# Expert gates by one rounded matmul a token, with the weight split moved to VectorE

## The chip, the cores and the metric

The kernel runs on one core of a Trainium2 chip. Its time is the device time of one execution in microseconds (us). A core has TensorE (PE, with its weight loads as PEld), VectorE (DVE), ScalarE (ACT), GpSimd (POOL) and SyncE (SP, which only issues transfers here). Each engine works through its own instruction list in order and waits on semaphores for the others.

## The reference

Two transformer blocks on 512 tokens of width 1024, in float32. The change lies in the first block's expert layer (`peer`), which selects 16 of 16384 experts for each token and each of 8 heads and mixes them with softmax gates:

```python
def peer(h, w_query, sub_keys, u_tab, v_tab):
    q = rmsnorm((xt @ w_query).reshape(T, PEER_HEADS, 2, PEER_PK_DIM))
    s = jnp.einsum('thpd,pnd->thpn', q, sub_keys)
    s1, i1 = lax.top_k(s[:, :, 0], PEER_TOPK)
    s2, i2 = lax.top_k(s[:, :, 1], PEER_TOPK)
    cand = (s1[..., :, None] + s2[..., None, :]).reshape(T, PEER_HEADS, n_cand)
    cidx = (i1[..., :, None] * PEER_N_KEYS + i2[..., None, :]).reshape(T, PEER_HEADS, n_cand)
    best, pos = lax.top_k(cand, PEER_TOPK)
    eidx = jnp.take_along_axis(cidx, pos, axis=-1)
    gate = jax.nn.softmax(best, axis=-1)
    ...
        act = jax.nn.gelu(jnp.einsum('td,thkd->thk', xb, u_tab[ib])) * gb
        return jnp.einsum('thk,thkd->td', act, v_tab[ib])
```

An expert's number is a pair of keys (i1, i2), each below 128, so one token's gates form a 128 x 128 table with at most 128 filled places.

## The kernel before, in words

The kernel computes the layer densely: gelu(x U) for all 16384 experts, times the token's table of gates, times V. Weights come in slabs of 128 x 2048 float32 (1 MB). `WStream` loads a slab (`wr`, three buffers), ScalarE rounds it (`wh`, line 295, a type whose matmul takes one pass), and a second engine, `lo_eng`, subtracts to get the rest (`wl`, line 302). A product of two float32 matrices is then three rounded matmuls (lines 307 to 309). `get` hands out a slab and splits the one two further on, so in each engine's list the split of slab i+2 stands right before the work of slab i.

The stretch in question is in `phase_peer`, after the queries. 42 of the 64 U slabs (the list `EARLY`) are multiplied there, ahead of the expert stage, and gelu of the result (`he`, line 1282) is stored to `d_h`. Beside them runs `route`, which finds the experts and builds the tables. The rest of the slabs and all V slabs are the stage after it.

`route` is a generator of small steps. `choose(t)` takes 128 tokens: for each of 8 heads a sum of 256 candidates and two rounds of MAX8, FIND_INDEX8 and MATCH_REPLACE8 on VectorE (lines 1463 to 1470), then a look-up of the keys, in which VectorE makes a mask (line 1496), GpSimd multiplies (line 1498) and VectorE reduces (line 1491), and a transpose into `ttt`. `spread(q)` takes four tokens: VectorE writes one one-hot mask for the first key of four tokens in one instruction (`oa`, line 1535) and four masks times gate for the second key (`ob`, line 1537). `place` follows two spreads later: four float32 matmuls into the PSUM tile `psc` (line 1525; a float32 matmul is two passes in the profile, so eight records), and ScalarE copies the 128 x 4 x 128 result into `gs` with the token innermost (line 1526), where consecutive elements of a token lie 128 bytes apart. Eight groups of four fill a 2 MB block that goes to `d_g`.

How the steps mix with the gemms is set by a count. `between` is called eight times a slab; from the 25th call on it takes steps from `route` until the sum of the numbers that they yield reaches its share of a total. 42 slabs are 336 calls. A yielded number is a weight in that share, nothing that is waited for. VectorE does no split in this stretch: `lo_eng` is GpSimd from the queries to the end of `route`.

Of the kernel before, what the change touches and what calls it, by code (L numbers as in the profile page):

```python
# [24 lines left out]
TT = S // 128  # L25
RMS_EPS = 1e-6
DN_ALPHA = 4.0 ** 0.25
EARLY = [i for i in range(64) if i % 4 and i not in (2, 26, 38, 46, 54, 62)]

# [247 lines left out]
class Builder:  # L277
# [913 lines left out]
    def phase_peer(self):  # L1191
# [4 lines left out]
        hh, hl = self.h2h, self.h2l  # L1196
        with ExitStack() as c:
            rp = c.enter_context(self.pool(name="rt_s", bufs=1))
            pp = c.enter_context(self.pool(name="rt_p", bufs=2, space=PSUM))
            iota = rp.tile([128, 128], F32, name="iota")  # L1200
            nc.scalar.dma_start(out=iota, in_=A["iota"])
            val = rp.tile([128, 4, 16, 16], F32, name="val")
# [2 lines left out]
            ws.lo_eng = "pool"  # L1205
            with ExitStack() as cq:
                tp = cq.enter_context(self.pool(name="rt_q", bufs=3))
                kT = rp.tile([128, 2, 128], F32, name="kT")
                nc.scalar.dma_start(out=kT, in_=A["pkT"].rearrange("p (a n) -> p a n", a=2))

                def rank(t, blk, sc):

                    a, b = val[:, t, blk, 0:8], val[:, t, blk, 8:16]
                    nc.vector.max(a, sc)
                    nc.vector.max_index(idx[:, t, blk, 0:8], a, sc)
                    nc.vector.match_replace(sc, a, sc, -3.0e38)
                    nc.vector.max(b, sc)
                    nc.vector.max_index(idx[:, t, blk, 8:16], b, sc)

                def turned(t, qd, q):  # L1220
                    pt = pp.tile([128, 4, 128], F32, name="pt", tag="pt")
                    for b in range(4):
                        nc.tensor.transpose(pt[:, b], q[:, b * 128:(b + 1) * 128], self.ident)
                    qT = tp.tile([128, 4, 128], F32, name="qT", tag="qT")
                    nc.scalar.copy(qT, pt)
                    return t, qd, qT

                def score(t, qd, qT):
                    ps = pp.tile([128, 4, 128], F32, name="psc", tag="psc")
                    for b in range(4):  # L1230
                        nc.tensor.matmul(ps[:, b], qT[:, b], kT[:, b % 2], start=True, stop=True)
                    sc = tp.tile([128, 4, 128], F32, name="sc", tag="sc")
                    nc.scalar.copy(sc, ps)
                    for b in range(4):
                        rank(t, 4 * qd + b, sc[:, b])

                q1, q2 = [], []
                for n in range(18):
                    qd, t = divmod(n, 4)
                    if n < 16:  # L1240
# [16 lines left out]
                    if q2:  # L1257
                        score(*q2.pop())
                    if q1:
                        q2.append(turned(*q1.pop()))  # L1260
                    if n < 16:
                        q1.append((t, qd, q))
            work, total = self.route(c, val, idx, ss, iota, pp)
            hp = c.enter_context(self.pool(name="rt_h", bufs=3))
            spent, n = 0.0, 0

            def between():
# [15 lines left out]
                    nc.sync.dma_start(out=self.d_h[2 * i + m], in_=h)  # L1283
            for _ in work:
                pass
            ws.lo_eng = "dve"
        self.late = ExitStack()
        yp = self.late.enter_context(self.pool(name="ex_y", bufs=1, side="right"))
        y = self.y1 = [yp.tile([128, 1024], F32, name=f"py{t}") for t in range(4)]
# [146 lines left out]
            c = max(a, 1)  # L1436
            nc.vector.tensor_tensor(xx[:, k4, c:b], xT[:, k4, c - 1:b - 1], xT[:, k4, c:b], op=OP.subtract)

    def route(self, ctx, val, idx, ss, iota, pp):


        nc = self.nc
        V, G = nc.vector, nc.gpsimd
        sp = ctx.enter_context(self.pool(name="ro_s", bufs=1))
        gp = ctx.enter_context(self.pool(name="ro_g", bufs=2))
        op_ = ctx.enter_context(self.pool(name="ro_o", bufs=4))
        rs = sp.tile([128, 4, 16], F32, name="rs16")
        nc.scalar.activation(rs, ss, AF.Ln, bias=self.eps_col(RMS_EPS), scale=1.0 / 128)
        nc.scalar.activation(rs, rs, AF.Exp, scale=-0.5)
# [2 lines left out]
        def choose(t):  # L1452
# [50 lines left out]
            for p in pend:  # L1503
                reduce(*p)
            yield 1.2 if t else 16.0
            pt = pp.tile([128, 4, 128], F32, name="pt", tag="pt")
# [3 lines left out]
            V.tensor_copy(tt, pt[:, 0:3])  # L1510
            tts[t] = tt
            yield 0.5

        queue = []
        blocks = {}

        def place():

            q, oa, ob = queue.pop(0)
            if q % 8 == 0:  # L1520
                blocks[q // 8] = gp.tile([128, 128, 32], F32, name="gs", tag="gs")
            gs = blocks[q // 8]
            pg = pp.tile([128, 4, 128], F32, name="psc", tag="psc")
            for r in range(4):
                nc.tensor.matmul(pg[:, r], ob[:, r], oa[:, r], start=True, stop=True)  # L1525
            nc.scalar.copy(gs[:, :, q % 8 * 4:q % 8 * 4 + 4].rearrange("p i t -> p t i"), pg)  # L1526
            if q % 8 == 7:
                nc.sync.dma_start(out=self.d_g[q // 8], in_=blocks.pop(q // 8))

        def spread(q):  # L1530
            tt = tts[q // 32]
            k = q % 32 * 4
            oa = op_.tile([128, 4, 128], F32, name="oa", tag="oa")
            ob = op_.tile([128, 4, 128], F32, name="ob", tag="ob")
            V.tensor_tensor(oa, iota.unsqueeze(1).to_broadcast([128, 4, 128]), tt[:, 0, k:k + 4].unsqueeze(2).to_broadcast([128, 4, 128]), op=OP.is_equal)
            for r in range(4):
                V.tensor_scalar(ob[:, r], iota, tt[:, 1, k + r:k + r + 1], tt[:, 2, k + r:k + r + 1], op0=OP.is_equal, op1=OP.mult)  # L1537
            queue.append((q, oa, ob))
            if len(queue) > 2:
                place()  # L1540

        def steps():
            yield from choose(0)
            for t in range(4):
                nxt = choose(t + 1) if t < 3 else iter(())
                debt = 0.0
                for q in range(32 * t, 32 * t + 32):
                    spread(q)
                    yield 1.65
                    debt += choice / 30  # L1550
                    while debt > 0:
                        d = next(nxt, None)
# [1293 lines left out]
```

## Time and profile before

| | us |
|---|---|
| median of 3 runs (3848.15 to 3857.06) | 3848.38 |
| the profiled execution | 3849.59 |
| its span, first to last instruction | 3847.8 |
| TensorE busy | 3694.6 (96%) |
| VectorE busy | 2321.1 (60%) |
| ScalarE busy | 1502.9 (39%) |
| GpSimd busy | 893.5 (23%) |
| mean granted TensorE clock | 0.984 of full speed |

The profile counts an engine busy from the start to the recorded end of an instruction. Instructions overlap at their ends, so for a sum the distance from one start to the next is the better number, and recorded durations are a little longer than that. The stretch of `route` runs from about 830 to 1408 us of the span.

### The profile page before, as it was taken

To read this page: it belongs to the slowest core of one execution; us is meant where nothing else is said; L and a number is where in the kernel's file an instruction comes from. 1 tells how busy PE (TensorE), PEld (TensorE's weight loads), DVE (VectorE), ACT (ScalarE), POOL (GpSimd) and SP (SyncE) were. 2 spreads that over 40 slices of the span, in tenths; PEclk is the share of its full clock that TensorE was granted. 3 is DMA by queue.
4 is the path that set the end of the run, shared out by engine and by line. 5 is a ranking of instruction groups with operands and counts; after the bars stand their busy time and mean duration, and the time that the engine had idled before them with its cause. 6 is when DMAs were issued, how large, how long until landed. Compare 5 with 4: busy or idle time off the path is not lost.

```text
span 3847.8 us, 49975 instructions
## 1 busy us (share of the span) xinstructions
PE 3694.6 (96%) x19452; PEld 3030.4 (79%) x19456; DVE 2321.1 (60%) x4075; ACT 1502.9 (39%) x2171; POOL 893.5 (23%) x500
## 2 busy tenths in 40 slices
PE   8999999899999999999999998998889998799999
PEld 4788867788888888888888887787778886688887
DVE  3564374696999863443434437873665547856455
ACT  3322284543544543322232324663333324443232
POOL 1201162335443431221221211233420000211000
PEclk9999999999999999999999999999999999899999
DMA  6376564224445566664655643469735221352231
GB/s 251 111 286 194 166 163 145 87 94 153 167 170 177 192 190 180 172 159 140 181 138 157 167 132 122 149 176 269 189 128 150 84 89 67 118 179 99 99 107 58
DMA packets 485884, 582.32 MB, mean 151 GB/s; under 512 B 339824, under 2 KB 381680, under 8 KB 448016
## 3 DMA queue, kind: packets, MB, share of 16 engines
q1 hardware_dynamic: 479744, 568.06, 48.4%
q10 hardware_dynamic: 5904, 11.08, 0.8%
q8 instruction: 153, 2.51, 0.3%
q14 instruction: 83, 0.68, 0.1%
HBM read 456.37 MB, written 121.63 MB: 150 GB/s over the span
## 4 chain that ended last, share of the span: by engine, by line
PE 82%; DVE 11%; ACT 3%; DMA 2%; issue 1%; SPq 1%; POOL 0%; ACTq 0%; DVEq 0%; POOLq 0%
PE acc L307 15%; PE acc L309 15%; PE acc L308 14%; PE pv L307 8%; PE pv L309 8%; PE pv L308 8%; PE psc L1525 3%; PE dpo L2778 1%; PE pz L2075 1%; DVE ob L1537 1%; PE acc L644 1%; PE rps L1833 1%; PE pvp L307 1%; PE pvp L309 1%; PE pvp L308 1%
## 5 line engine op out<-in xcount | busy, mean ns | idle before, releaser
L295 ACT CAST wh<-wr 128x2048 fp32r<-128x2048 f32 (+2 forms) x310 | 510.2, 1665 | 378.2 <-PE pv L309 270.3
L302 DVE TENSOR_TENSOR wl<-wr,wh 128x2048 fp32r<-128x2048 f32 (+2 forms) x236 | 478.6, 2048 | 168.7 <-ACT wh L295 168.5
L308 PE MATMUL pv<-wl,ah 128*128 128x512 f32 x1376 | 535.8, 389 | 1.8 <-DVE wl L302 1.8
L307 PE MATMUL pv<-wh,ah 128*128 128x512 f32 x1376 | 537.0, 390 | 0.4 <-ACT wh L295 0.4
L309 PE MATMUL pv<-wh,al 128*128 128x512 f32 x1376 | 536.0, 390 | 0.0
L302 POOL TENSOR_TENSOR wl<-wr,wh 128x2048 fp32r<-128x2048 f32 (+1 forms) x80 | 333.5, 4176 | 536.7 <-ACT wh L295 508.5
L307 PE MATMUL acc<-h2h,wh 128*128 128x512 f32 x1024 | 412.8, 403 | 0.0
L309 PE MATMUL acc<-h2h,wl 128*128 128x512 f32 x1024 | 402.9, 393 | 0.0
L308 PE MATMUL acc<-h2l,wh 128*128 128x512 f32 x1024 | 399.2, 390 | 0.0
L308 PEld LDWEIGHTS pv<-wl,ah 128*128 128x128 f32 x1376 | 258.6, 188 | 56.4 <-DVE wl L302 2.4
L307 PEld LDWEIGHTS pv<-wh,ah 128*128 128x128 f32 x1376 | 258.6, 188 | 54.7 <-ACT wh L295 0.9
L309 PEld LDWEIGHTS pv<-wh,al 128*128 128x128 f32 x1376 | 258.4, 188 | 54.2
L307 PE MATMUL acc<-xth,wh 128*128 128x512 f32 (+1 forms) x768 | 288.3, 375 | 0.7 <-ACT xth L295 0.7
L309 PE MATMUL acc<-xth,wl 128*128 128x512 f32 (+1 forms) x768 | 286.6, 373 | 0.0
L308 PE MATMUL acc<-xtl,wh 128*128 128x512 f32 (+1 forms) x768 | 284.3, 370 | 1.1 <-DVE xtl L302 1.1
L1376 DVE TENSOR_TENSOR py<-py,pv 128x512 f32<-128x512 f32 x119 | 80.4, 685 | 319.7 <-PE pv L309 319.7
L1537 DVE TENSOR_SCALAR ob<-iota,ttt 128x128 f32<-128x128 f32 x512 | 239.7, 533 | 0.0
L309 PEld LDWEIGHTS acc<-h2h,wl 128*128 128x128 f32 x1024 | 192.1, 188 | 43.1
L1526 ACT COPY gs<-psc 128x512 f32<-128x512 f32 x128 | 143.3, 1120 | 210.5 <-PE psc L1525 207.2
L308 PEld LDWEIGHTS acc<-h2l,wh 128*128 128x128 f32 x1024 | 192.9, 188 | 38.6
L307 PEld LDWEIGHTS acc<-h2h,wh 128*128 128x128 f32 x1024 | 192.9, 188 | 35.4
L302 POOL TENSOR_TENSOR al<-cv,ah 128x512 fp32r<-128x512 f32 x44 | 57.0, 1295 | 633.3 <-ACT ah L295 570.5
(601 smaller groups left out, 7260.4 us busy)
## 6 DMA issues: line engine op xcount, KB each, us to landing
wr<-in_pu SPq DMA_DIRECT2D x64, 1024.0 KB, 5.5
wr<-in_pv SPq DMA_DIRECT2D x64, 1024.0 KB, 5.6
wr<-in_f_up SPq DMA_DIRECT2D x44, 1024.0 KB, 5.0
d_g<-gs SPq DMA_DIRECT2D x16, 2048.0 KB, 10.4
gt<-d_g SPq DMA_DIRECT2D x128, 256.0 KB, 5.7
d_h<-he SPq DMA_DIRECT2D x84, 256.0 KB, 5.3
hs<-d_h SPq DMA_DIRECT2D x84, 256.0 KB, 5.0
wadb<-in_ada_b SPq DMA_DIRECT2D x32, 512.0 KB, 6.4
```

The source lines that it names most:

```text
L295: nc.scalar.copy(hi, src)
L302: (nc.vector if le == "dve" else nc.gpsimd).tensor_tensor(lo, src, hi.bitcast(F32), op=OP.subtract)
L307: mm(ps, w[0], x[0], start=first, stop=False)
L308: mm(ps, w[0], x[1], start=False, stop=False)
L309: mm(ps, w[1], x[0], start=False, stop=last)
L644: nc.tensor.matmul(ps[0:2], sc[:, 4 * half + k], w[:, k], start=(half + k == 0), stop=(half == 1 and k == 3))
L1376: nc.vector.tensor_tensor(yt, yt, ps, op=OP.add)
L1525: nc.tensor.matmul(pg[:, r], ob[:, r], oa[:, r], start=True, stop=True)
L1526: nc.scalar.copy(gs[:, :, q % 8 * 4:q % 8 * 4 + 4].rearrange("p i t -> p t i"), pg)
L1537: V.tensor_scalar(ob[:, r], iota, tt[:, 1, k + r:k + r + 1], tt[:, 2, k + r:k + r + 1], op0=OP.is_equal, op1=OP.mult)
L1833: nc.tensor.matmul(ps[:, i * 256 + hp * 128:i * 256 + hp * 128 + 128], f2(bk[:, 2 * q + i, hp:hp + 2]), ar[:, hp, :, 2 * q + i], start=Tru ...
L2075: nc.tensor.matmul(p[rows[hp], j], l[:, j, h64], r[:, j, h64] if r.shape[2] == 128 else r[:, j], start=True, stop=True)
```

## The change

- `oa` of a token becomes 256 columns of the rounded type: 128 hold the mask of the first key times the gate's rounded part `gh` (four VectorE instructions a group, line 1558), 128 hold the same times the ratio of rest to rounded part (four ScalarE instructions, line 1559). `ob` becomes a plain mask (one VectorE instruction, line 1560). `place` does four rounded matmuls of 256 columns.
- The two halves have to be added. ScalarE copies the low half to `gw` (line 1537), and in the next spread VectorE adds high half and `gw` into `gs` (`gather`, line 1546), in the same layout as before.
- `choose` gets five small VectorE instructions that make `gh` and the ratio.
- In the stretch, `lo_eng` is VectorE; GpSimd keeps only the multiply of the look-up.
- `EARLY` has 45 slabs (26, 46 and 62 are added), so there are 360 calls of `between`; a spread yields 1.9, not 1.65.
- Buffers: `psc` takes two banks a tile and the transposes use `acc`; `oa`, `ob` and `eq` have three buffers, not four, `he` has two, not three.

```diff
-EARLY = [i for i in range(64) if i % 4 and i not in (2, 26, 38, 46, 54, 62)]
+EARLY = [i for i in range(64) if i % 4 and i not in (2, 38, 54)]
...
-            work, total = self.route(c, val, idx, ss, iota, pp)
-            hp = c.enter_context(self.pool(name="rt_h", bufs=3))
+            ws.lo_eng = "dve"
+            work, total = self.route(c, val, idx, ss, iota)
+            hp = c.enter_context(self.pool(name="rt_h", bufs=2))
...
+            gh = sp.tile([128, 128], F32R, name="gh", tag="gh", bufs=2)
+            V.tensor_copy(gh, tt[:, 2])
+            gh = gh.bitcast(F32)
+            gl = sp.tile([128, 16, 16], F32, name="v", tag="v").rearrange("p a k -> p (a k)")[:, 0:128]
+            V.tensor_tensor(gl, tt[:, 2], gh, op=OP.subtract)
+            V.tensor_scalar(tt[:, 2], gh, 1.0e-30, None, op0=OP.max)
+            V.reciprocal(tt[:, 2], tt[:, 2])
+            V.tensor_tensor(tt[:, 2], gl, tt[:, 2], op=OP.mult)
...
             q, oa, ob = queue.pop(0)
+            pg = pp.tile([128, 4, 2, 128], F32, name="psc", tag="psc")
+            for r in range(4):
+                nc.tensor.matmul(pg[:, r], ob[:, r], oa[:, r], start=True, stop=True)
+            lo = op_.tile([128, 4, 128], F32, name="gw", tag="gw", bufs=2)
+            nc.scalar.copy(lo, pg[:, :, 1])
+            sums.append((q, pg, lo))
+
+        def gather():
+
+            q, pg, lo = sums.pop(0)
...
-            pg = pp.tile([128, 4, 128], F32, name="psc", tag="psc")
-            for r in range(4):
-                nc.tensor.matmul(pg[:, r], ob[:, r], oa[:, r], start=True, stop=True)
-            nc.scalar.copy(gs[:, :, q % 8 * 4:q % 8 * 4 + 4].rearrange("p i t -> p t i"), pg)
+            V.tensor_tensor(gs[:, :, q % 8 * 4:q % 8 * 4 + 4].rearrange("p i t -> p t i"), pg[:, :, 0], lo, op=OP.add)
...
-            V.tensor_tensor(oa, iota.unsqueeze(1).to_broadcast([128, 4, 128]), tt[:, 0, k:k + 4].unsqueeze(2).to_broadcast([128, 4, 128]), op=OP.is_equal)
+            if sums:
+                gather()
             for r in range(4):
-                V.tensor_scalar(ob[:, r], iota, tt[:, 1, k + r:k + r + 1], tt[:, 2, k + r:k + r + 1], op0=OP.is_equal, op1=OP.mult)
+                V.tensor_scalar(oa[:, r, 0], iota, tt[:, 0, k + r:k + r + 1], gh[:, k + r:k + r + 1], op0=OP.is_equal, op1=OP.mult)
+                nc.scalar.activation(oa[:, r, 1], oa[:, r, 0].bitcast(F32), AF.Copy, scale=tt[:, 2, k + r:k + r + 1])
+            V.tensor_tensor(ob, iota.unsqueeze(1).to_broadcast([128, 4, 128]), tt[:, 1, k:k + 4].unsqueeze(2).to_broadcast([128, 4, 128]), op=OP.is_equal)
...
-                    yield 1.65
+                    yield 1.9
```

VectorE's list before, at the end of `route`: the last two groups of four tokens (`oa` and `ob`) and the first split of the next stage. The numbers behind the names tell buffers apart.

```order
L1535 TENSOR_TENSOR oa_11054<-iota_5196,ttt_10256 128x512 [waits PE_49]
L1537 TENSOR_SCALAR ob_11055<-iota_5196,ttt_10256 128x128 [waits DVE_49]
L1537 TENSOR_SCALAR ob_11055<-iota_5196,ttt_10256 128x128 x3
L1535 TENSOR_TENSOR oa_11077<-iota_5196,ttt_10256 128x512 [waits PE_49]
L1537 TENSOR_SCALAR ob_11078<-iota_5196,ttt_10256 128x128 [waits DVE_49]
L1537 TENSOR_SCALAR ob_11078<-iota_5196,ttt_10256 128x128 x3
L302 TENSOR_TENSOR wl_11165<-wr_10730,wh_11164 128x2048 [waits DMAHW7_49,Activation_49]
```

VectorE's list in the changed kernel, in the last slabs of `route`: `gs` is the gather, `wl` the split of a slab.

```order
L1558 TENSOR_SCALAR oa_11951<-iota_5193,ttt_10974,gh_10976 128x128 [waits DVE_49]
L1558 TENSOR_SCALAR oa_11951<-iota_5193,ttt_10974,gh_10976 128x128 x3
L1560 TENSOR_TENSOR ob_11952<-iota_5193,ttt_10974 128x512 [waits DVE_49]
L302 TENSOR_TENSOR wl_11974<-wr_11521,wh_11973 128x2048 [waits DMAHW5_49,Activation_49]
L1546 TENSOR_TENSOR gs_11921<-psc_11963,gw_11968 128x4x128 [waits PE_49]
L1558 TENSOR_SCALAR oa_11992<-iota_5193,ttt_10974,gh_10976 128x128 [waits DVE_49]
L1558 TENSOR_SCALAR oa_11992<-iota_5193,ttt_10974,gh_10976 128x128 x3
L1560 TENSOR_TENSOR ob_11993<-iota_5193,ttt_10974 128x512 [waits DVE_49]
```

A gather stands in each group now, and once a slab a `wl` that waits for ScalarE's `wh`; before, neither of the two stood in this stretch of VectorE's list. From the first instruction of `choose(0)` to the last gather there are 41 such `wl`, four of them ahead of the first spread. Of the other 37, 25 stand right behind an `ob`, 7 behind a head of `choose` that follows one, 4 behind a mask and a reduction (lines 1497 and 1492 of the changed kernel) and one behind a mask alone. Of the 128 gathers 54 stand right behind an `ob`.

ScalarE's list before, near the end of `route`: the copies `gs`, gelu of half a slab (`he`) and the rounding of a slab (`wh`).

```order
L1526 COPY gs_10962<-psc_10982 128x4x128 [waits PE_49]
L1282 ACTIVATE he_10994<-acc_10942 128x512 [waits DMAHW1_49,PE_49,Activation_49]
L295 CAST wh_10997<-wr_10603 128x2048 [waits DMAHW4_49,Pool_49]
L1526 COPY gs_10962<-psc_11017 128x4x128 [waits PE_49]
L1526 COPY gs_10962<-psc_11036 128x4x128 [waits PE_49]
```

ScalarE's list in the changed kernel, at the place of VectorE's rows above: `oa` are the low halves, `gw` the copy of the low results.

```order
L1559 ACTIVATE oa_11951<-oa_11951,ttt_10974 128x128 [waits DVE_49] x4
L1537 COPY gw_11968<-psc_11963 128x512 [waits PE_49,Activation_49]
L1283 ACTIVATE he_11970<-acc_11886 128x512 [waits DMAHW3_49]
L295 CAST wh_11973<-wr_11521 128x2048 [waits DMAHW5_49]
L1559 ACTIVATE oa_11992<-oa_11992,ttt_10974 128x128 [waits DVE_49] x4
```

The rounding `wh_11973`, which VectorE's `wl_11974` waits for, now stands behind `gw` and `he`, and these stand behind four instructions that each wait for a mask `oa_11951` of VectorE.

## Rows read from the trace of the kernel before

**Rows 1.** The page: busy times of the engines; the chain that ended last.

```profile
PE 3694.6 (96%) x19452; PEld 3030.4 (79%) x19456; DVE 2321.1 (60%) x4075; ACT 1502.9 (39%) x2171; POOL 893.5 (23%) x500
PE 82%; DVE 11%; ACT 3%; DMA 2%; issue 1%; SPq 1%; POOL 0%; ACTq 0%; DVEq 0%; POOLq 0%
```

**Rows 2.** Windows: length; busy PE, PEld, DVE, ACT, POOL; clock; DMA.

```profile
830.00:1410.00 580.00, 579.57 (x3055) 494.28 (x3054) 513.14 (x1096) 277.81 (x270) 243.95 (x74) 1.00 0.49 170
1410.00:2310.00 900.00, 897.74 (x3953) 740.44 (x3953) 369.54 (x323) 258.21 (x263) 171.51 (x127) 1.00 0.60 161
...
2400.00:2425.00 25.00, 20.67 (x87) 15.97 (x87) 18.58 (x29) 15.26 (x25) 0.00 (x0) 1.00 0.30 104
```

**Rows 3.** One piece of the chain of waits: start, us, what.

```profile
932.22 0.89 PE psc L1525 x8
```

**Rows 4.** Timeline of TensorE in the route stretch: start, us, instruction.

```profile
1101.60 0.39 PE L308 MATMUL acc<-h2l,wh 128*128 128x512 f32 x1
1101.83 0.39 PE L309 MATMUL acc<-h2h,wl 128*128 128x512 f32 x1
```

**Rows 5.** Timeline of TensorE in an earlier stage, rounded matmuls of 256 columns.

```profile
344.59 0.28 PE L307 MATMUL pc<-hch,wh 128*128 128x256 f32 x1
344.71 0.28 PE L308 MATMUL pc<-hcl,wh 128*128 128x256 f32 x1
```

**Rows 6.** One line's and one tile's instructions: ns min/median/max, first and last start.

```profile
L1535 DVE TENSOR_TENSOR oa<-iota,ttt x128: 672/687/5006, 915.9 to 1398.6; 128x512 f32<-128x512 f32 x128
L1282 ACT ACTIVATE he<-acc x84: 597/599/670, 834.0 to 1407.7; 128x512 f32<-128x512 f32 x84
```

**Rows 7.** Timeline of VectorE, two spreads and the start of the third.

```profile
1306.01 0.68 DVE L1535 TENSOR_TENSOR oa<-iota,ttt 128x512 f32<-128x512 f32 x1
1306.61 1.11 DVE L1537 TENSOR_SCALAR ob<-iota,ttt 128x128 f32<-128x128 f32 x4
1307.63 0.69 DVE L1535 TENSOR_TENSOR oa<-iota,ttt 128x512 f32<-128x512 f32 x1
```

**Rows 8.** Timeline of VectorE and of GpSimd, the same instructions beside a GpSimd split.

```profile
929.56 5.40 DVE L1537 TENSOR_SCALAR ob<-iota,ttt 128x128 f32<-128x128 f32 x4
...
929.75 4.62 POOL L302 TENSOR_TENSOR wl<-wr,wh 128x2048 fp32r<-128x2048 f32 x1 [6.74 <-ACT wh L295]
```

**Rows 9.** Timeline of VectorE, the first instruction of two heads of `choose(0)`.

```profile
848.43 0.41 DVE L1463 TENSOR_TENSOR eq<-v 128x256 f32<-128x256 f32 x1
851.26 0.41 DVE L1463 TENSOR_TENSOR eq<-v 128x256 f32<-128x256 f32 x1
```

**Rows 10.** Groups by line, 820 to 1412 us: busy us, mean ns, idle before.

```profile
L1496 DVE TENSOR_TENSOR eq<-iota,jf 128x512 f32<-128x512 f32 x32 | 24.3, 763 | 0.0
L1491 DVE TENSOR_REDUCE tr<-eq 128x32 f32<-128x512 f32 x32 | 21.4, 678 | 17.5 <-POOL eq L1498 17.5
L1498 POOL TENSOR_TENSOR eq<-eq,fi 128x512 f32<-128x512 f32 x32 | 46.8, 1476 | 33.2 <-DVE eq L1496 27.0 <-PE psc L1525 4.0 <-DMA d_h<-he 2.3
L295 ACT CAST wh<-wr 128x2048 fp32r<-128x2048 f32 x43 | 81.7, 1899 | 0.0
L1526 ACT COPY gs<-psc 128x512 f32<-128x512 f32 x128 | 143.3, 1120 | 210.5 <-PE psc L1525 207.2 <-issue 3.3
```

**Rows 11.** Groups by line over the whole run, for comparison.

```profile
L1225 ACT COPY qT<-pt 128x512 f32<-128x512 f32 x16 | 9.4, 587 | 0.0
L1982 DVE TENSOR_TENSOR tmp<-U,Y 128x576 f32<-128x576 f32 x1 | 1.2, 1203 | 0.0
L1376 DVE TENSOR_TENSOR py<-py,pv 128x512 f32<-128x512 f32 x119 | 80.4, 685 | 319.7 <-PE pv L309 319.7
L1256 ACT ACTIVATE jk<-q 128x128 bf16<-128x128 f32 x64 | 19.8, 310 | 2.0
```

**Rows 12.** VectorE's splits in 1410 to 2300 us: durations; who ended its idle time.

```profile
L302 DVE TENSOR_TENSOR wl<-wr,wh x82: 2278/2287/3331, 1410.2 to 2294.8; 128x2048 fp32r<-128x2048 f32 x82
...
  ACT wh L295: 95.1, 33
```

More of the change, by code (lines that the diff above doesn't have):

```diff
@@ L1198, in phase_peer @@
             rp = c.enter_context(self.pool(name="rt_s", bufs=1))
-            pp = c.enter_context(self.pool(name="rt_p", bufs=2, space=PSUM))
             iota = rp.tile([128, 128], F32, name="iota")
@@ L1207, in phase_peer @@
                 tp = cq.enter_context(self.pool(name="rt_q", bufs=3))
-                kT = rp.tile([128, 2, 128], F32, name="kT")
+                pp = cq.enter_context(self.pool(name="rt_p", bufs=2, space=PSUM))
+                kT = tp.tile([128, 2, 128], F32, name="kT", bufs=1)
                 nc.scalar.dma_start(out=kT, in_=A["pkT"].rearrange("p (a n) -> p a n", a=2))
@@ L1285, in phase_peer @@
                 pass
-            ws.lo_eng = "dve"
         self.late = ExitStack()
@@ L1437, in shift_turn, with route @@
             nc.vector.tensor_tensor(xx[:, k4, c:b], xT[:, k4, c - 1:b - 1], xT[:, k4, c:b], op=OP.subtract)
-    def route(self, ctx, val, idx, ss, iota, pp):
+    def route(self, ctx, val, idx, ss, iota):
         nc = self.nc
@@ L1445, in route @@
         gp = ctx.enter_context(self.pool(name="ro_g", bufs=2))
-        op_ = ctx.enter_context(self.pool(name="ro_o", bufs=4))
+        op_ = ctx.enter_context(self.pool(name="ro_o", bufs=3))
+        pp = ctx.enter_context(self.pool(name="ro_p", bufs=2, space=PSUM))
         rs = sp.tile([128, 4, 16], F32, name="rs16")
@@ L1505, in choose @@
             yield 1.2 if t else 16.0
-            pt = pp.tile([128, 4, 128], F32, name="pt", tag="pt")
+            pt = self.acc.tile([128, 4, 128], F32, name="acc", tag="acc")
             for a in range(3):
@@ L1510, in choose @@
             V.tensor_copy(tt, pt[:, 0:3])
+            gh = sp.tile([128, 128], F32R, name="gh", tag="gh", bufs=2)
[6 more added lines that the diff above has]
+            V.tensor_tensor(tt[:, 2], gl, tt[:, 2], op=OP.mult)
+            tt = tt, gh
             tts[t] = tt
@@ L1515, in route @@
         blocks = {}
+        sums = []
         def place():
             q, oa, ob = queue.pop(0)
+            pg = pp.tile([128, 4, 2, 128], F32, name="psc", tag="psc")
[6 more added lines that the diff above has]
+            q, pg, lo = sums.pop(0)
             if q % 8 == 0:
@@ L1530, in spread @@
         def spread(q):
-            tt = tts[q // 32]
+            tt, gh = tts[q // 32]
             k = q % 32 * 4
-            oa = op_.tile([128, 4, 128], F32, name="oa", tag="oa")
-            ob = op_.tile([128, 4, 128], F32, name="ob", tag="ob")
-            V.tensor_tensor(oa, iota.unsqueeze(1).to_broadcast([128, 4, 128]), tt[:, 0, k:k + 4].unsqueeze(2).to_broadcast([128, 4, 128]), op=OP.is_equal)
+            oa = op_.tile([128, 4, 2, 128], F32R, name="oa", tag="oa")
+            ob = op_.tile([128, 4, 128], F32R, name="ob", tag="ob")
+            if sums:
+                gather()
             for r in range(4):
-                V.tensor_scalar(ob[:, r], iota, tt[:, 1, k + r:k + r + 1], tt[:, 2, k + r:k + r + 1], op0=OP.is_equal, op1=OP.mult)
+                V.tensor_scalar(oa[:, r, 0], iota, tt[:, 0, k + r:k + r + 1], gh[:, k + r:k + r + 1], op0=OP.is_equal, op1=OP.mult)
+                nc.scalar.activation(oa[:, r, 1], oa[:, r, 0].bitcast(F32), AF.Copy, scale=tt[:, 2, k + r:k + r + 1])
+            V.tensor_tensor(ob, iota.unsqueeze(1).to_broadcast([128, 4, 128]), tt[:, 1, k:k + 4].unsqueeze(2).to_broadcast([128, 4, 128]), op=OP.is_equal)
             queue.append((q, oa, ob))
@@ L1558, in steps @@
             while queue:
+                if sums:
+                    gather()
                 place()
                 yield 0.9
+            gather()
+            yield 0.9
         choice = 0.6 + 16.0 + 1.6 + 8 * 1.2 + 1.2 + 0.5
-        return steps(), 4 * choice + 128 * 1.65 + 16.6
+        return steps(), 4 * choice + 128 * 1.9 + 16.6
     def phase_rwkv(self, d_src):
```

## The prediction

> **What bounds the kernel now.** I read the page first: TensorE is busy 96% of the span and makes up 82% of the chain of waits [rows 1], so the question at each stage is whether something else can become later than it. The windows show that in the stretch of `route` TensorE is busy 579.6 of 580 us, and VectorE 513, by far its fullest stage; in the stage after it TensorE is busy 897.7 of 900 us and VectorE only 370 [rows 2]. So the reader is to see two things: TensorE bounds both stages, and in the first VectorE has little left, about 67 us. Then I asked what fills VectorE there. The same four masks and gates that take 1.11 us alone take 5.40 us when a GpSimd split of 4.62 us runs beside them [rows 7, 8]: part of the 513 us is standing still beside GpSimd. Alone, a spread takes 1307.63 - 1306.01 = 1.62 us from start to start [rows 7].
>
> **What the change takes off TensorE.** One group of four tokens holds TensorE for 0.89 us [rows 3]. Rounded matmuls of 256 columns follow each other in 344.71 - 344.59 = 0.12 us [rows 5], so the new group costs 4 x 0.12 = 0.48 us. The saving is 128 x 0.41 = 52.5 us, if TensorE stays the bound. The three slabs that move cost 48 matmuls each at 1101.83 - 1101.60 = 0.23 us [rows 4], 11.0 us a slab, 33 us together: added to the first stage, taken from the second, nothing in sum while TensorE bounds both. Storing and fetching their six halves of h adds transfers to stages whose transfer engines are at 0.49 and 0.61 [rows 2]; I take that as hidden, and if the cover is gone it is late at the multiply by the gates in the second stage.
>
> **What it puts on VectorE.** The masks cost the same as before: four instructions with two scalars and one with 512 elements, in the other order, 1.62 us. That the four now write the rounded type is not shown by any row; I take no difference, bounded at 0 and, if they ran at one element a step, some 0.06 us each, 30 us in all.
>
> The gather is new: 128 x 512 elements from PSUM, written 128 bytes apart. Written in order, such an addition takes 685 ns [rows 11]. Against that, ScalarE's copy into the same layout takes 1120 ns where a copy of this size in order takes 587 ns [rows 10, 11], and VectorE's product that reads one operand in steps of 256 bytes takes 1203 ns for 576 elements, that is (1203 - 152)/576 = 1.82 ns an element, with 152 ns fixed as what 685 ns leaves at 1.04 ns an element [rows 11]. At 1.82 ns, 512 elements take 1.08 us; instructions overlap by some 0.08 us (0.68 against a distance of 0.60 in rows 7), so 1.00 us. Bounds: 0.60 and 1.15 us. I take 1.00, since both rows with such steps say so.
>
> The Trainium skill has a rule that speaks against this part of the change: "SBUF — State Buffer", section "Door 1: The DMA port swizzle", says that SBUF works in lines of 16 bytes and that each access that goes to a new line pays. By the page alone every element of the gather would pay, without a figure for how much; without the rule the gather would be 0.60 us, and the forecast below 128 x 0.40 = 51 us lower. The 1120 ns of ScalarE agree with the rule.
>
> The splits move to VectorE at 2.29 us each, about 2.2 from start to start [rows 12]. In return it no longer stands still for GpSimd's splits; GpSimd keeps 32 multiplies of 1.48 us [rows 10], which I let cost 0.5 us each, between 0 and 1.4.
>
> **The sum for the first stage.** Its gemms begin at about 828 (the first gelu at 834.0 less half a slab, 5.5), and the last gelu is at 1407.7 [rows 6]. The steps before the first spread yield 44.3 of a total of 377.8, so the count puts it at call 24 + 44.3 x 336/377.8 = 63, that is 7.9 slabs or 87 us in, at 915, where it is today (915.9, rows 6). VectorE reaches it about then: `choose(0)` begins behind the split that waits for slab 3, at 828 + 33 + 5 = 866 (gelu, rounding and split, 0.6 + 1.9 + 2.2), and needs 34 us and four splits, 43 together, plus some 5 us of waiting for the exponential. With the five new instructions I take 918.
>
> From there VectorE has to do:
> - 128 spreads at 1.62: 207 us;
> - 128 gathers at 1.00: 128 us;
> - three times `choose`: 8 heads at 851.26 - 848.43 = 2.83 [rows 9], 8 masks and 8 reductions at about 0.6 each from start to start (763 ns with the stalls, and 678) [rows 10], 2 us of small ones, together 34.3; with 2.4 for the transposed copy and the new five, 110 us;
> - 37 splits at 2.2: 81 us;
> - 24 multiplies on GpSimd beside it: 12 us.
>
> That is 538 us and ends at 1456. TensorE's own work ends much sooner: 828 + 45 x 11.0 + 128 x 0.48 + 3 for the transposes = 1387. VectorE is the bound, and TensorE waits for masks.
>
> **The added wait.** Behind an `ob`, the split `wl` waits for ScalarE, which after VectorE's last mask still has to do one low half (0.31 us), `gw` (0.59), `he` (0.60) and the rounding `wh` (1.90) [rows 6, 10, 11]. With the starts overlapping, `wh` ends about 3.6 us after the last mask started, and VectorE, done with `ob` 0.86 us after that start, stands for 2.8 us. Behind the waiting `wl` the next gather and masks are queued, and for those TensorE waits. 25 of 37 splits stand so: 70 us; four behind a mask and a reduction wait 1.6 us, 6 us more. The 54 gathers right behind an `ob` wait for `gw` some 0.4 us each: 22 us. So the waits are between 0 and 98 us. The nearest row is the stage after: there 82 VectorE splits waited 95.1 us for ScalarE's rounding, 33 times [rows 12], 1.16 us a split. With that, 37 splits wait 43 us; the gathers I take at half, 11. The stage then ends at 1456 + 54 = 1510, that is 102 us after today's 1408.
>
> The second stage loses three slabs and stays bound by TensorE: -33 us. The profiled execution becomes 3849.6 + 102 - 33 = 3919, and the median lies 1.2 us below it in this kernel, so I say 3918.
>
> **The rivals.**
> 1. VectorE bounds the stage, but ScalarE runs far enough ahead that nothing waits. For it: ScalarE was busy only 278 of 580 us [rows 2]. Against it: its list is in order, and the low halves tie it to VectorE's masks. The stage ends at 1456: 3849.6 + 48 - 33 = 3865.
> 2. VectorE bounds it and every wait is paid in full: 1456 + 98 = 1554, 3963. For it: the order of the two lists; against it: the 1.16 us of the next stage.
> 3. TensorE stays the bound, or nearly: the gather costs as much as an addition written in order, 0.60 us a start, and the waits vanish. VectorE then needs 487 us and ends at 1405: 3849.6 - 3 - 33 = 3814; the floor is 52.5 us below today, 3797. It decides where VectorE needs less than 1387 - 918 = 469 us, or 3.7 us a group with everything in it. For it: an engine other than ScalarE may write such steps faster; against it: the steps cost VectorE as much in reading as they cost ScalarE in writing [rows 10, 11].
>
> A lower TensorE clock would change little: with its 469 us from 918 to 1387 spread over the 592 us until 1510 TensorE is busy about 0.79 of the time, and a window with 20.67 of 25 us busy still shows a clock of 1.00 [rows 2].
>
> **How the numbers follow.** The forecast (3885 to 3945) has 0.49, rival 1 (3850 to 3880) 0.18, rival 2 (3945 and above) 0.15, rival 3 (below 3850) 0.18. What a measurement of this kernel can tell from no change is about 0.3%, 11.5 us: 3837 to 3860. Rival 1 gives that 0.05 of its chance and rival 3 0.01 of its own; so faster 0.17, same 0.06, slower 0.77. The range leaves out the lowest part of rival 3 and the uppermost of rival 2, each about a tenth: 3808 to 3972.
>
> **What would show it.** In the profile after, the 1408 of the last gelu moves to about 1510, VectorE is busy above nine tenths from 918 on, and the chain of waits in that stretch goes over VectorE rather than TensorE. The gather has a mean near 1.08 us; 0.69 would speak for rival 3. GpSimd's 4.6 us splits are gone and a spread takes 1.62 us throughout. VectorE's idle time before `wl` names ScalarE's `wh`, about 43 us; near 0 it is rival 1, above 70 rival 2. The new group of matmuls costs 0.48 us. The second stage is 33 us shorter. The forecast is wrong if TensorE has no gaps in the first stage, or if the second stage does not give the 33 us back because h from memory comes late.

## The result and the profile after

The changed kernel takes 3969.25 us (median of five runs, 3963.3 to 3974.95), 1.0307 times the kernel before [1.0296, 1.0318]: slower by 121 us, where 70 were forecast. That is rival 2's part of the range (3945 and above, given 0.15), not the forecast's (3885 to 3945). Its profiled execution took 3963.3 us. The first stage now ends at 1551.2 us, 143.5 later than before, and what follows it lasts 2410.3 us instead of 2440.1. Both differences together, 143.5 - 29.8, are the whole 113.7 between the two profiled executions. The end of the first stage is the start of the last gelu of the early slabs.

Two lines of the changed kernel, with the columns of [rows 6]: gelu at the end of a half slab, and the gather.

```profile
L1283 ACT ACTIVATE he<-acc x90: 577/592/607, 832.0 to 1551.2; 128x512 f32<-128x512 f32 x90
L1546 DVE TENSOR_TENSOR gs<-psc,gw x128: 995/1074/1140, 934.7 to 1551.3; 128x512 f32<-128x512 f32 x128
```

The page's busy times, which answer to [rows 1]: GpSimd lost its splits, TensorE has 508 records fewer (four a group would be 512), ScalarE gained 79 us.

```profile
PE 3691.8 (93%) x18944; PEld 2998.0 (76%) x18944; DVE 2386.3 (60%) x4265; ACT 1582.0 (40%) x2683; POOL 695.4 (18%) x458
```

Windows of the changed kernel, with the columns of [rows 2]: the first stage from the first spread on, and the stage behind it.

```profile
918.00:1551.00 633.00, 516.12 (x2280) 414.20 (x2279) 517.16 (x1108) 334.98 (x758) 31.05 (x24) 0.93 0.39 143
1551.00:2420.00 869.00, 866.79 (x3811) 715.02 (x3810) 360.62 (x319) 247.98 (x253) 167.94 (x125) 1.00 0.62 164
```

Nobody is full in the first line: TensorE is busy 82% of it, VectorE 82%, ScalarE 53%. That is the mark of engines that wait for each other in turn. The second line is like before: TensorE at 1.00 clock and without gaps.

VectorE's groups in that first window (busy us, mean ns | idle before, and who ended it):

```profile
L1558 DVE TENSOR_SCALAR oa<-iota,ttt,gh 128x128 fp32r<-128x128 f32 x508 | 140.3, 340 | 0.0
L1546 DVE TENSOR_TENSOR gs<-psc,gw 128x512 f32<-128x512 f32 x128 | 136.7, 1069 | 27.7 <-ACT gw L1537 27.7
L1560 DVE TENSOR_TENSOR ob<-iota,ttt 128x512 fp32r<-128x512 f32 x127 | 86.9, 685 | 0.0
L302 DVE TENSOR_TENSOR wl<-wr,wh 128x2048 fp32r<-128x2048 f32 x37 | 84.8, 2292 | 83.6 <-ACT wh L295 83.6
```

All of VectorE's waiting stands in two of these lines: 83.6 us before 35 of its 37 splits (2.4 each) and 27.7 us before 57 gathers. Together 111.3 of 633 us; the other 522 are its own work. The buffers that the change gave up explain none of it: VectorE has no wait for a free `oa` or `ob`, and ScalarE's waits for a free `he`, 31.5 us, all lie ahead of 918, while the first spread still begins at 916.2 (915.9 before).

One such wait behind an `ob`, first in VectorE's timeline, with the idle time before an instruction in brackets, then in ScalarE's:

```profile
1475.80 1.11 DVE L1546 TENSOR_TENSOR gs<-psc,gw 128x512 f32<-128x512 f32 x1 [0.45 <-ACT gw L1537]
1476.75 1.08 DVE L1558 TENSOR_SCALAR oa<-iota,ttt,gh 128x128 fp32r<-128x128 f32 x4
1477.75 0.69 DVE L1560 TENSOR_TENSOR ob<-iota,ttt 128x512 fp32r<-128x512 f32 x1
1481.18 2.29 DVE L302 TENSOR_TENSOR wl<-wr,wh 128x2048 fp32r<-128x2048 f32 x1 [2.74 <-ACT wh L295]
1483.38 1.01 DVE L1546 TENSOR_TENSOR gs<-psc,gw 128x512 f32<-128x512 f32 x1
1484.25 1.09 DVE L1558 TENSOR_SCALAR oa<-iota,ttt,gh 128x128 fp32r<-128x128 f32 x4
```

```profile
1477.10 1.28 ACT L1559 ACTIVATE oa<-oa,ttt 128x128 fp32r<-128x128 f32 x4 [1.33 <-DVE oa L1558]
1478.29 0.56 ACT L1537 COPY gw<-psc 128x512 f32<-128x512 f32 x1
1478.75 0.59 ACT L1283 ACTIVATE he<-acc 128x512 f32<-128x512 f32 x1
1479.24 1.90 ACT L295 CAST wh<-wr 128x2048 fp32r<-128x2048 f32 x1
1484.60 1.28 ACT L1559 ACTIVATE oa<-oa,ttt 128x128 fp32r<-128x128 f32 x4 [3.46 <-DVE oa L1558]
```

ScalarE waits 1.33 us for VectorE's mask at 1476.75, then works through low halves, `gw`, `he` and `wh`; VectorE is done with `ob` and waits 2.74 us for `wh`; then ScalarE waits 3.46 us for VectorE's next mask. Each is idle while the other works. A split behind a head of `choose` waits too, here 1.65 us:

```profile
966.56 2.29 DVE L302 TENSOR_TENSOR wl<-wr,wh 128x2048 fp32r<-128x2048 f32 x1 [1.65 <-ACT wh L295]
```

The chain of waits from 1466 to 1486 us, around the first of these splits, alternates in the same way, and TensorE is not in it:

```profile
by line: ACT oa L1559 31.4%; DVE gs L1546 21.3%; ACT gw L1537 14.3%; DVE wl L302 11.5%; ACT wh L295 9.1%; issue 8.2%; DVE oa L1558 5.0%; ACT he L1283 2.5%; ACTq L1283 0.1%
```

TensorE's timeline shows the part that did what it should: the new group and the gemm's next matmul in the changed kernel, then (apart) the same place before.

```profile
1152.84 0.64 PE L1535 MATMUL psc<-oa,ob 128*128 128x256 f32 x4
1153.31 0.40 PE L307 MATMUL acc<-h2h,wh 128*128 128x512 f32 x1
1153.54 0.40 PE L308 MATMUL acc<-h2l,wh 128*128 128x512 f32 x1
```

```profile
1199.94 1.05 PE L1525 MATMUL psc<-oa,ob 128*128 128x128 f32 x8
1200.75 0.48 PE L307 MATMUL acc<-h2h,wh 128*128 128x512 f32 x1
1201.07 0.39 PE L308 MATMUL acc<-h2l,wh 128*128 128x512 f32 x1
```

A group costs 0.47 us from its start to the next gemm matmul. Before it was 0.81, and the gemm matmul behind it took 0.32 instead of 0.23 from start to start: 0.90 in all.

### The profile page after: what moved, and what is told of

It is laid out like the page before. It is cut to its first block, busy times and chain, and to the rows that moved or that the text cites. A ratio compares the mean times of both kernels' runs of the same rounds, so it can differ in the third digit from the quotient of the medians.

```text
span 3961.5 us, 49623 instructions
## 1 busy us (share of the span) xinstructions
PE 3691.8 (93%) x18944; PEld 2998.0 (76%) x18944; DVE 2386.3 (60%) x4265; ACT 1582.0 (40%) x2683; POOL 695.4 (18%) x458
## 4 chain that ended last, share of the span: by engine, by line
PE 66%; DVE 19%; ACT 9%; issue 3%; DMA 2%; POOL 1%; SPq 0%; ACTq 0%; DVEq 0%; POOLq 0%
PE acc L307 11%; PE acc L309 11%; PE acc L308 11%; PE pv L309 8%; PE pv L307 8%; PE pv L308 8%; DVE gs L1546 2%; ACT oa L1559 2%; DVE wl L302 2%; ACT wh L295 2%; DVE oa L1558 1%; ACT gw L1537 1%; PE dpo L2805 1%; PE pz L2102 1%; PE acc L644 1%
## 5 line engine op out<-in xcount | busy, mean ns | idle before, releaser
L302 DVE TENSOR_TENSOR wl<-wr,wh 128x2048 fp32r<-128x2048 f32 (+2 forms) x278 | 570.7, 2070 | 261.2 <-ACT wh L295 261.0
L309 PE MATMUL acc<-h2h,wl 128*128 128x512 f32 x1024 | 413.1, 403 | 0.0
L308 PE MATMUL acc<-h2l,wh 128*128 128x512 f32 x1024 | 411.0, 401 | 0.0
L1559 ACT ACTIVATE oa<-oa,ttt 128x128 fp32r<-128x128 f32 x512 | 163.9, 391 | 289.8 <-DVE oa L1558 289.8
L307 PEld LDWEIGHTS acc<-h2h,wh 128*128 128x128 f32 x1024 | 201.0, 196 | 37.6
L302 POOL TENSOR_TENSOR al<-hs,ah 128x512 fp32r<-128x512 f32 x90 | 121.1, 1367 | 507.0 <-ACT ah L295 507.0
L1535 PE MATMUL psc<-oa,ob 128*128 128x256 f32 x512 | 92.4, 306 | 113.1 <-DVE gs L1546 111.0
L1535 PEld LDWEIGHTS psc<-oa,ob 128*128 128x128 f32 x512 | 78.8, 201 | 143.4 <-issue 113.5
```

The costliest lines, as they stand in the source:

```text
L302: (nc.vector if le == "dve" else nc.gpsimd).tensor_tensor(lo, src, hi.bitcast(F32), op=OP.subtract)
L307: mm(ps, w[0], x[0], start=first, stop=False)
L308: mm(ps, w[0], x[1], start=False, stop=False)
L309: mm(ps, w[1], x[0], start=False, stop=last)
L1559: nc.scalar.activation(oa[:, r, 1], oa[:, r, 0].bitcast(F32), AF.Copy, scale=tt[:, 2, k + r:k + r + 1])
```

## The experiments

The theory: VectorE bounds the first stage, and on top of its own work it stands for ScalarE's rounding and copies. The rivals were that only the load counts and not the waits, that the choice of engine for the splits counts, and that the matmuls gain nothing. The runs were made on three chips, on which the kernel before took 3856.82, 3851.45 and 3855.04 us (medians), so each is compared by its ratio to the kernel before on the same chip; a step of 0.001 is about 3.9 us. The intervals of the first four runs are about 10 us to either side.

### The split later in VectorE's list

Same work; the subtraction, and with it the order to load a further slab, is only issued some calls of `between` after ScalarE's rounding, so that other VectorE work stands between.

```diff
+        if self.defer:
+            self.B.split(t[:, :n], h[:, :n], None, self.hi_eng)
+            self.later.append((t[:, :n], h[:, :n], l[:, :n], more))
...
+                if n % 8 == 4:
+                    ws.flush()
```

> The changed kernel, but VectorE's split of a slab (wl) stands half a slab later in its list, behind the fourth of the eight step calls, so that ScalarE's rounding is long done; the same instructions otherwise. Theory (VectorE's list bounds the first stage, and in the changed kernel it stood 91 us for the rounding): those 91 us fall below 15, the gathers that stood behind a split now wait some 0.45 us each, 10 us more, so the stage ends 70 us earlier and the time is about 3897 us (3880 to 3915). Rival (the waits of VectorE are spare time, TensorE's hand-over of PSUM tiles or its lower clock sets the pace): the waits vanish and the time stays within 12 us of 3969.

Measured: 3883.34 us, ratio 1.0069 [1.0044, 1.0094], against 1.0307. The first stage ends at 1471.4. The window and VectorE's waits (total us, times, longest) of that run:

```profile
916.00:1471.00 555.00, 494.36 (x2296) 399.59 (x2296) 520.54 (x1115) 333.08 (x760) 35.18 (x24) 0.98 0.46 163
```

```profile
DVE gs L1565 <- ACT gw L1556: 29.5, 57, 1.3
DVE ttt L1530 <- PE acc L1528: 0.4, 1, 0.4
```

VectorE's work is the same 520 us; the 83.6 us before `wl` are gone, and the stage is 82 us shorter (637.4 from first to last gelu, 719.2 before the edit). By ratio 0.0238 of the 0.0307 came back; the plain medians, 3969.25 and 3883.34, are 86 of 121 us apart. So seven to eight tenths of the loss are waits that depend on the place in the list alone. VectorE, now busy 94%, is the bound in the plain sense.

### The gather written in order

```diff
-            gs = blocks[q // 8]
-            V.tensor_tensor(gs[:, :, q % 8 * 4:q % 8 * 4 + 4].rearrange("p i t -> p t i"), pg[:, :, 0], lo, op=OP.add)
+            gs = blocks[q // 8].rearrange("p i t -> p (i t)")[:, q % 8 * 512:q % 8 * 512 + 512].rearrange("p (t i) -> p t i", t=4)
+            V.tensor_tensor(gs, pg[:, :, 0], lo, op=OP.add)
```

In this and in the later run of the same edit the gates of a block come out permuted.

> The changed kernel, but the gather writes its 512 elements in order instead of 128 bytes apart, so the block goes to memory in another order (the gates are permuted). Theory (steps of 128 bytes cost 0.4 us a gather on a VectorE that bounds the stage): the gather falls from 1.07 to 0.69 us and the time by 128 x 0.4 = 51 us to about 3918 (3905 to 3930). Rival (the gather's length is hidden, only its wait for ScalarE counts): the gather falls as well, and the time stays within 12 us of 3969.

Measured: 3936.77 us, 1.0202 [1.0177, 1.0227]; the stage ends at 1524.4. VectorE's groups from 918 to 1525 us:

```profile
L1546 DVE TENSOR_TENSOR gs<-psc,gw 128x512 f32<-128x512 f32 x128 | 87.6, 685 | 28.6 <-ACT gw L1537 28.6
L1560 DVE TENSOR_TENSOR ob<-iota,ttt 128x512 fp32r<-128x512 f32 x128 | 87.5, 684 | 0.0
L302 DVE TENSOR_TENSOR wl<-wr,wh 128x2048 fp32r<-128x2048 f32 x38 | 87.1, 2291 | 84.7 <-ACT wh L295 84.7
```

The direction holds, the size doesn't. The gather falls to 685 ns, but its cost with 128-byte steps was not 1.00 us from start to start: the timelines of the changed kernel show 0.84 to 0.96, mean 0.91, against 0.60 in order, as here:

```profile
1158.51 0.69 DVE L1546 TENSOR_TENSOR gs<-psc,gw 128x512 f32<-128x512 f32 x1 [0.44 <-ACT gw L1537]
1159.12 1.11 DVE L1558 TENSOR_SCALAR oa<-iota,ttt,gh 128x128 fp32r<-128x128 f32 x4
```

That is 128 x 0.31 = 39 us, not 51; the time fell by 0.0105, about 40 us (33 from median to median). The waits stay as they were (113.3 us, 111.3 before the edit), so VectorE's work and waits add up here.

### The splits back on GpSimd

```diff
-            ws.lo_eng = "dve"
...
+            ws.lo_eng = "dve"
```

(The second line stands at the end of `route` again.)

> The changed kernel, but GpSimd splits the slabs in the first stage, as before. Theory (the gather is what VectorE cannot carry, and taking the splits costs it about what standing beside GpSimd cost): VectorE has 207 us of masks, 128 of gathers, 110 of choosing, and stands about 37 x 4 = 150 us beside GpSimd, with 24 us of waits for gw, in all 620; the stage ends near 1540 and the time stays within 25 us of 3969. Rival (moving the splits to VectorE, with its 81 us of work and 91 us of waits, is the cause): the time falls by over 100 us, to 3850 or below.

Measured: 3934.8 us, 1.0198 [1.0171, 1.0226], 0.0109 or about 42 us faster than the changed kernel (34 from median to median). Groups from 918 to 1523 us, VectorE's masks and GpSimd's splits:

```profile
L1558 DVE TENSOR_SCALAR oa<-iota,ttt,gh 128x128 fp32r<-128x128 f32 x512 | 252.2, 556 | 0.0
L302 POOL TENSOR_TENSOR wl<-wr,wh 128x2048 fp32r<-128x2048 f32 x37 | 178.9, 4836 | 345.5 <-ACT wh L295 345.5
```

The masks take 112 us more because VectorE stands still beside GpSimd's splits, as in [rows 8]. But VectorE no longer has 85 us of splits, nor 84 us of waiting in front of them: GpSimd does the waiting, and nothing is queued behind it. Neither kernel comes near the one before, so where the splits are is not the main cause. Moving them did cost 34 to 42 us of the 121, more than the 25 that I had allowed, so neither the theory nor the rival (over 100) was right in size.

### The sum made in PSUM, without a gather

The halves are summed by a second matmul into the same columns, and ScalarE copies the result as before. It takes 128 VectorE gathers away and gives TensorE four matmuls more a group.

```diff
-                nc.tensor.matmul(pg[:, r], ob[:, r], oa[:, r], start=True, stop=True)
+                nc.tensor.matmul(pg[:, r], ob[:, r], oa[:, r, 0], start=True, stop=False)
+                nc.tensor.matmul(pg[:, r], ob[:, r], oa[:, r, 1], start=False, stop=True)
...
+            nc.scalar.copy(gs[:, :, q % 8 * 4:q % 8 * 4 + 4].rearrange("p i t -> p t i"), pg)
```

> The changed kernel without the gather: the two halves are added by TensorE, eight rounded matmuls of 128 columns a group that accumulate in pairs in one PSUM tile, and ScalarE copies it with steps of 128 bytes as in the kernel before. Splits on VectorE, 45 slabs. Theory (VectorE's list with the gather is the bound): VectorE's need after 918 falls from 633 to 410 and some 80 us of waits, 490, the stage ends near 1410, and the time is about 3828 us; if a rounded matmul of 128 columns takes as long as a pass of a float32 one (0.11 us), TensorE ends at 1440 and it is about 3858. Rival (the waits of the splits alone slow the stage, the gather is covered): the time stays above 3930.

Measured: 3886.66 us, 1.0072 [1.0046, 1.0098]. The first two and the last rows of one group on TensorE and what follows:

```profile
1330.65 0.22 PE L1535 MATMUL psc<-oa,ob 128*128 128x128 f32 x1
1330.71 0.28 PE L1536 MATMUL psc<-oa,ob 128*128 128x128 f32 x1
...
1331.38 0.27 PE L1536 MATMUL psc<-oa,ob 128*128 128x128 f32 x1
1331.49 0.45 PE L307 MATMUL acc<-h2h,wh 128*128 128x512 f32 x1
1331.78 0.39 PE L308 MATMUL acc<-h2l,wh 128*128 128x512 f32 x1
```

Eight rounded matmuls of 128 columns take 0.84 us, and the gemm matmul behind them 0.29: with the 0.06 over its usual 0.23 that is 0.90, exactly what eight float32 passes cost before. So this form had nothing to gain on TensorE, and both of my times were too low. TensorE was busy 538.9 of the 557 us from 916 to 1473, and VectorE waited 124 us:

```profile
DVE wl L302 <- ACT wh L295: 124.0, 37, 5.8
```

That these waits are what the form still lost, the later run of it (below) bears out.

### One part alone in the kernel before

VectorE's splits without the new matmuls:

```diff
+            ws.lo_eng = "dve"
             work, total = self.route(c, val, idx, ss, iota, pp)
```

> The kernel before with one part of the change alone: VectorE instead of GpSimd splits the slabs beside the route. Theory: VectorE then has 128 x 1.62 + 110 + 81 = 398 us of work after the first group, TensorE 492 us, so TensorE stays the bound and waits of VectorE for ScalarE's rounding fit into the 94 us that are left: 3848, 3838 to 3860. Rival (the wait costs the stage whatever else VectorE has to do): some 90 us more, 3940.

Measured: 3851.17 us, 0.9995 [0.9985, 1.0004]. The window, and the splits in VectorE's groups from 916 to 1410 us:

```profile
916.00:1408.00 492.00, 491.61 (x2668) 422.65 (x2667) 407.15 (x971) 245.60 (x238) 32.37 (x25) 1.00 0.50 179
```

```profile
L302 DVE TENSOR_TENSOR wl<-wr,wh 128x2048 fp32r<-128x2048 f32 x35 | 81.2, 2320 | 77.0 <-ACT wh L295 76.8
```

VectorE's waits for `wh` in that window (total us, times, longest):

```profile
DVE wl L302 <- ACT wh L295: 76.8, 28, 6.5
```

This is the run that puts the waits in their place. VectorE stands before `wl` for 77 us, nearly as long as in the changed kernel, and the time doesn't move: TensorE is busy 491.6 of 492 us. Here a wait cost nothing, because VectorE did not bound the stage.

Three more slabs beside `route`, without the new matmuls: `EARLY` of the changed kernel in the kernel before.

> The kernel before with another part alone: 45 slabs instead of 42 beside the route. Theory (TensorE bounds both stages there, a slab only changes its place): 3848, 3838 to 3858, first stage 33 us later. Rival (moving slabs is itself a gain, as it is in the changed kernel): 3822 to 3830.

Measured: 3856.26 us, 1.0009 [0.9999, 1.0018]; the stage ends at 1443.6. Its window:

```profile
836.00:1443.00 607.00, 607.00 (x3177) 517.25 (x3176) 534.98 (x1073) 279.05 (x274) 258.98 (x77) 1.00 0.49 169
```

TensorE is without a gap in it, and the slabs only change their place, as the theory has it.

### More slabs beside the late split

If VectorE bounds the stage, TensorE's gaps there can take slabs from the stage behind. 48 and 54 slabs, and 53 with slab 2 left where it was; this is the edit for 54:

```diff
-EARLY = [i for i in range(64) if i % 4 and i not in (2, 38, 54)]
+EARLY = [i for i in range(64) if i % 4 or i in (8, 16, 24, 40, 48, 56)]
```

> The late split of the first experiment with 48 slabs beside the route instead of 45. In that run VectorE was busy 588 of the stage's 637 us and TensorE some 60 to 75 us short of filled. Theory (VectorE bounds the stage, so a slab moved into it costs VectorE one split, 2.2 us, and takes 11 us out of the stage after): 3883 + 3 x 2.2 - 3 x 11 = 3857, 3845 to 3868, first stage ending near 1478. Rival (TensorE bounds it, so a slab only changes its place): 3883 as with 45, first stage ending near 1504.

> The same with 54 slabs. Theory: 3883 + 9 x 2.2 - 9 x 11 = 3804, but TensorE's own work in the stage is by then about as long as VectorE's, and its floor is 3797 (52 us below the kernel before), so 3804 to 3830; that is faster than the kernel before (3848). Rival (a slab only changes its place): 3883.

> The run with 54 slabs, but slab 2 stays in the stage after. With it gone, TensorE was busy only 36 or 37 of the first 50 us of that stage with 48 and 54 slabs, while with 45 it was busy 98 of 100. Theory (the gap comes from slab 2, whose gemm covers the start of the stage): the 14 us come back, a slab fewer costs 5: 3870 - 14 + 5 = 3861, 3852 to 3867. Rival (the gap comes from the transfers whatever the slab): 3870 to 3880.

Measured: 3880.05 us, 1.0069 [1.0052, 1.0086], with 48; 3869.89, 1.0046 [1.0031, 1.0061], with 54; 3859.96, 1.0018 [1.0009, 1.0028], with 53. The first two miss my theory by 23 and about 40 us. With 48 the ratio is the same as with 45, 1.0069, so the time is the rival's, although the stage ended at 1486.5, at neither's mark (1478, 1504). The stage grew by 13.0 us for three slabs and 37.6 for nine, 4.2 a slab where I had put 2.2. The stage behind gave back only 20 us for three, where 33 were expected. The start of that stage with 48 slabs, and with 53:

```profile
1486.00:1536.00 50.00, 35.89 (x142) 28.25 (x142) 20.05 (x18) 18.27 (x23) 15.62 (x12) 0.83 0.93 220
```

```profile
1505.00:1555.00 50.00, 48.47 (x213) 39.60 (x212) 23.88 (x17) 19.75 (x26) 15.50 (x12) 1.00 0.97 232
```

With slab 2 moved TensorE is idle there for 14 us; with it back the gap is gone and the run lands on the 3861 expected of it. Of the rest I can only say that TensorE and VectorE are both nearly full by then: with 53 slabs they are busy 97% and 92% of the time from 916 to 1503 us. Why a slab costs 4.2 us is not settled.

### Gather removed, cheapened or summed, all with the late split

Without the sum: ScalarE copies the high half to `gs` and the low half is left out.

```diff
-            lo = op_.tile([128, 4, 128], F32, name="gw", tag="gw", bufs=2)
-            nc.scalar.copy(lo, pg[:, :, 1])
-            sums.append((q, pg, lo))
...
+            nc.scalar.copy(gs[:, :, q % 8 * 4:q % 8 * 4 + 4].rearrange("p i t -> p t i"), pg[:, :, 0])
```

> The late split, and no sum of the halves: ScalarE copies the high half straight into the block of gates (the low half of the gates is left out of the result; masks, low halves and the 256-column matmuls all stay). VectorE then has 538 - 128 = 410 us of work from 918 on, TensorE 469. Theory (VectorE was the bound, the matmuls themselves are worth their 52 us): the first stage ends at 1387 to 1395, 3797 to 3806 in all. Rival (the matmuls gain nothing, or ScalarE's low halves hold the stage as well): 3848 and more.

Measured: 3806.93 us, 0.9878 [0.9861, 0.9894].

```profile
916.00:1385.00 469.00, 468.68 (x2288) 393.36 (x2287) 415.63 (x988) 389.30 (x759) 31.30 (x24) 1.00 0.54 193
```

TensorE is full again, the last gelu is at 1387.7, the 1387 that the prediction gave as TensorE's own end. The matmul part is worth nearly what it was said to be worth, 0.0122 or 47 us of the 52.5; the sum on VectorE and the waits are what hide it.

> The late split and the gather written in order (the gates of a block come out permuted). The late split left the end of the stage at 1471, 15 us over VectorE's own work. Theory (VectorE's work and waits add up): 128 x 0.4 = 51 us less, stage end 1420, 3883 - 51 = 3832, 3815 to 3845. Rival (the gather in order gives only the 32 us that it gave with the early split): 3851.

Measured: 3853.07 us, 0.9997 [0.9988, 1.0007], so the rival's number. VectorE's waits from 918 to 1445 us:

```profile
DVE gs L1565 <- ACT gw L1556: 32.9, 59, 1.6
DVE ttt L1530 <- PE acc L1528: 6.4, 2, 5.2
```

The theory of adding up is not refuted, its term was: the gather saves 39 us, not 51, and VectorE waits 39.3 us instead of 29.9, partly for TensorE by now. 39 - 9 = 30, and the run is 0.0072, about 28 us, below the late split alone (30 from median to median).

> The late split and the sum made by TensorE: eight rounded 128-column matmuls of 0.11 us a group into one tile, no gather; a candidate that computes all of the gates. Its early-split form took 3887 with 157 us of splits waiting for ScalarE. Theory (those waits were what it lost): TensorE's group is 0.84 instead of 0.89 us, 6 us less than the kernel before, 3842, 3838 to 3856. Rival (TensorE filled already, the waits cost nothing there): 3880 to 3890.

Measured: 3855.99 us, 1.0009 [0.9999, 1.0018], 0.0063 or about 24 us less than with the early split (31 from median to median).

```profile
916.00:1440.00 524.00, 524.00 (x2805) 448.13 (x2805) 410.49 (x987) 397.49 (x759) 31.07 (x24) 1.00 0.48 172
```

TensorE is busy every one of the 524 us. With a group at 0.90 us as before, equal to the kernel before is all that it could be; my 0.84 had left out what the group costs the matmul behind it. Of the versions of the change that put all of the gates in their places this has the lowest ratio, though the late split with 53 slabs (1.0018) is not clear of it, and none beats the kernel before.

## Why the prediction came out as it did

The direction and the engine were right; one term, the wait, was half of what came. The time lies outside the forecast's own band, and within the stated range (3808 to 3972) by less than 3 us: that it is inside owes something to the 16 us that VectorE's work was put too high.

- **The bound moves to VectorE.** Right. In the slab shown the chain runs over VectorE and ScalarE, TensorE has gaps, and removing VectorE work or waits shortens the stage, while in the kernel before the same wait costs nothing (0.9995).
- **VectorE's own work, 538 us.** 522 from 918 on. The gather's distance to the next instruction was 0.91 us, not 1.00: 128 x 0.09 = 12 of the 16 us; the other 4 are not traced. Its recorded median, 1.074 (mean 1.069), is what was expected: I took too little off the recorded duration for the overlap.
- **The added wait, taken as 54 between 0 and 98.** This is the term that was mis-sized: 111. The working behind the 98 was right almost to the row. 25 splits behind an `ob` were put at 2.8 us and wait 2.74 (68.5 us in all); four behind a mask and a reduction were put at 1.6 and wait 1.54. The gathers were put at 22 us and wait 27.7. The other eight splits, behind a head of `choose` or a mask, were put at nothing without a reason, and they wait 8.9 us. What was wrong was to go from there to the nearest row, the 1.16 us a split of the second stage [rows 12]. That is an average over 82 splits of which 33 waited, 2.9 us each on average, and the other 49 not at all. Here 35 of 37 waited, 2.4 us each: a single wait was no longer than there, but it came nearly every time. The two lists suggest why: the four low halves tie ScalarE to VectorE's masks in each group, so that ScalarE can't run ahead. No run takes the low halves alone away, so this stays an argument. They are not needed for such waits: in the kernel before with VectorE's splits ScalarE has no low halves, and 28 of 35 splits still waited, 76.8 us.
- **The sum.** 918 + 522 + 111 = 1551, rival 2's end of 1554. The excess over the forecast's 1510 is +57 of waits and -16 of work.
- **The second stage, -33.** -29.8 in the profiled execution, with TensorE busy 866.8 of 869 us. (The transfer engines' 0.61 in the prediction is 0.60 in [rows 2]; nothing hangs on it.)
- **TensorE's own end, 1387; a group, 0.48 us.** Right: 0.47, and 1387.7 in the run without the sum.
- **VectorE busy above nine tenths.** Wrong: 538 of the forecast's 592 us would have been 0.91, but with twice the wait it is 0.82. It is 0.94 once the split stands later.
- **The clock.** It fell to 0.93 in the stage, where TensorE was busy 82%, though a window busy 83% had shown 1.00 [rows 2]. This didn't decide: VectorE's work and its waits for ScalarE fill the stage, and none of its waits there is for TensorE. With the late split the clock was 0.98, and the stage is shorter by what VectorE's waits lost, 82 us against 83.6.

By ratio, of the 0.031 that the change lost, 0.024 came back with the split at another place in the list; 0.007 more with the gather in order; a further 0.012, now a gain, when the sum went altogether. The last two kernels are no replacements: one permutes the gates and the other leaves out their low half.

## What to carry to other kernels

When work moves to an engine, write out what stands ahead of the instruction it waits for, in the other engine's list too. If that list hangs on the first engine's own last instruction, the wait is the sum of what stands between, less what the first engine has left to do, and it can come each time; an average over a stage in which most splits met no wait is no guide. A wait is only worth its length on the bounding engine, and there the cure may be cheaper than the work: here the same instruction some calls later in the list gave back seven to eight tenths of the loss.

## What the hardware showed that I had not expected

- A rounded matmul of 128 columns takes 0.11 us from start to start, one of 256 columns 0.12. Eight of the narrow ones cost as much as eight float32 passes; only the wide form, one for two halves, made TensorE's part cheaper.
- A group of narrow matmuls also delays the 512-column matmul behind it, 0.29 to 0.32 us to the next start instead of 0.23; behind the 256-column ones it was 0.23.
- An addition that writes in 128-byte steps has a recorded median of 1074 ns against 685 ns in order, but only 0.31 us more from start to start.
